# Joining two down projections into one accumulation, and taking two weight scales from column norms

## The chip, the core and the metric

The kernel runs on one core of one Trainium2 chip. The metric is device time in microseconds from one launch to its end, the median of three runs. One further execution was taken with the hardware profiler, and all rows shown below are from it. The engines are named as the profile names them: PE is TensorE (PEld its weight loads), DVE is VectorE, ACT is ScalarE, POOL is GpSimd, and SP is the engine whose queue issues nearly all DMAs here (SPq).

## What is computed

One layer of a pre-normalised residual block over 2048 tokens of width 1024, in float32, with two attention branches (differential attention with 4 heads, stick-breaking attention with 8) and a SwiGLU feed-forward part of 2816 features:

```python
u = rms_norm(h, norm1_w[l])
proj = jnp.einsum('bsd,de->bse', u, w_in[l])
...
h = h + jnp.einsum('bse,ed->bsd', mix, w_out[l])
u2 = rms_norm(h, norm2_w[l])
gate = jnp.einsum('bsd,df->bsf', u2, w_gate[l])
up = jnp.einsum('bsd,df->bsf', u2, w_up[l])
h = h + jnp.einsum('bsf,fd->bsd', jax.nn.silu(gate) * up, w_down[l])
```

The change lies in the last four lines, and in how the operands of `gate` and `up` are prepared.

## The kernel before, in words

Float32 accuracy comes from 16-bit matmuls: each operand is scaled by a power of two and split into a high and a low f16 part, and a product is three matmuls (high·high, high·low, low·high).

The first phase (0 to about 1474 us) does the normalisation, the input projection, both attentions and the output projection. `out_proj` takes the 16 token tiles (128 tokens each) one after the other: 96 matmuls of 128x256 into `po`, the residual is added (`xf`), and the sum goes to the DRAM tensor `hd`. For tiles 0 to 7, `post` also normalises the tile, transposes it on PE, and `x_ops` forms the seven operands X of the next phase, which go to the DRAM tensor `xcd`.

The second phase (1474 to 2866 us) is the feed-forward part: two halves of 1024 tokens, and in each 11 groups of 256 features, so 22 steps. A 2x2 block product is done Strassen-Winograd fashion, with seven block products in place of eight. Step i does on PE

- gate(i): seven products of 12 matmuls of 128x512 (`quad`, `product`), whose results ACT and DVE turn into silu values (tiles `cg`);
- down(i-1): for each of four pairs of token tiles (the loop over `j`), seven products of three matmuls, 84 in all, into PSUM tiles `pd`. DVE adds each one, scaled by `kd`, into `cu` scratch or into the output tiles `hs` (`acc`), and POOL or DVE adds scratch to `hs` (`tt`);
- up(i): as gate, and at its end the seven operands of the next down, `act`, in high and low parts (a copy on ACT, a subtraction on POOL or DVE).

The output tiles `hs`, eight of 128x1024 float32, stay in SBUF through a half: they are loaded from `hd` once, and stored to `out` in its last down.

The weights of a step (`g`, `u`, `d`: 1 MB each) are loaded in float32 into the tag `fst` (two buffers), combined in place on POOL, and split into f16 (`load_ffn`, `split_weight`): high parts on ACT or POOL, low parts on DVE. Gate and up weights share the tag `wgu` (two buffers), `wd` has one. In half 0 each weight first gets its scale from its data. For `g` and `u` that is a maximum of absolute values over 2048 columns on DVE (L190). For `d` it is a sum of squares on ACT (L187), written to the `wd` tile as junk. The 128 partition results are spread by a small float32 matmul into `fsc` (`across`, L179) and reduced once more on DVE. Half 1 uses the scales again. `build_x` makes the X operands of half 1 piece by piece in the downs of half 0 (the `ticks`), in buffers `bx` and `fst`.

The order of the instructions on each engine comes from a scheduler that simulates the program with its buffers, in the order in which the code emits it; `pick` gives a piece of work to the engine that has been given least by `note`. Each engine then runs its own queue in that order, so what waits at a queue's head holds up all behind it.

## Time and profile before

| | |
|---|---|
| median of three runs | 2863.46 us (2859.81 to 2869.82) |
| the profiled execution, its own time | 2867.49 us |
| its span, first to last instruction | 2865.7 us |
| mean granted TensorE clock | 0.957 |
| PE busy | 2510.0 us (88%) |
| DVE busy | 2399.3 us (84%) |
| POOL busy | 1847.9 us (64%) |
| ACT busy | 1469.5 us (51%) |
| gate(0) starts | 1477.07 us |
| first up product of half 0, of half 1 | 1502.22 us, 2174.30 us |
| last down starts | 2838.45 us |

A busy engine in this profile need not be at its peak, and the share of a whole span is an average over stages. The two halves of the feed-forward part show this: the same 252 matmuls per step take 67.2 us in half 0 ((2174.30 − 1502.22) / 10) and 58.05 us in half 1, where no scales are computed and no X operands are built.

### The profile page before, as it was taken

To read this page: it belongs to the slowest core of one execution; us is meant where nothing else is said; L and a number is where in the kernel's file an instruction comes from. 1 tells how busy PE (TensorE), PEld (TensorE's weight loads), DVE (VectorE), ACT (ScalarE), POOL (GpSimd) and SP (SyncE) were. 2 spreads that over 40 slices of the span, in tenths; PEclk is the share of its full clock that TensorE was granted. 3 is DMA by queue.
4 is the path that set the end of the run, shared out by engine and by line. 5 is a ranking of instruction groups with operands and counts; after the bars stand their busy time and mean duration, and the time that the engine had idled before them with its cause. 6 is when DMAs were issued, how large, how long until landed. Compare 5 with 4: busy or idle time off the path is not lost.

```text
span 2865.7 us, 45554 instructions
## 1 busy us (share of the span) xinstructions
PE 2510.0 (88%) x16888; PEld 1396.6 (49%) x16888; DVE 2399.3 (84%) x4152; ACT 1469.5 (51%) x2680; POOL 1847.9 (64%) x1258
## 2 busy tenths in 40 slices
PE   7998898988888777899888989888899999999997
PEld 4565555555555444477653434333344444444443
DVE  6888879787989999787548989889988888898887
ACT  4665656567777888656323433434334333433432
POOL 3567767664545555465427867767777887787775
PEclk9999999999999888999999989999999999999999
DMA  6778877879999898978951222323134511111111
GB/s 229 194 159 176 169 172 161 179 165 220 214 192 192 163 177 167 203 166 225 268 216 44 84 71 76 96 74 94 45 96 162 176 45 59 59 50 54 59 45 59
DMA packets 672224, 390.95 MB, mean 136 GB/s; under 512 B 532784, under 2 KB 622896, under 8 KB 670208
## 3 DMA queue, kind: packets, MB, share of 16 engines
q1 hardware_dynamic: 670176, 385.95, 55.2%
q8 instruction: 132, 2.16, 0.3%
q0 software_dynamic: 512, 1.36, 0.2%
q14 instruction: 92, 0.75, 0.1%
q10 hardware_dynamic: 1312, 0.72, 0.1%
HBM read 199.48 MB, written 49.02 MB: 87 GB/s over the span
## 4 chain that ended last, share of the span: by engine, by line
PE 21%; DVE 18%; POOL 7%; issue 6%; DMA 4%; ACT 2%; SPq 0%; DVEq 0%; POOLq 0%; ACTq 0%
PE pd L975 6%; PE pa L887 4%; PE pm L887 4%; DVE wu L210 4%; PE pd L887 4%; POOL hs L101 2%; POOL fst L101 2%; PE po L752 2%; DVE wg L210 2%; DVE cg L101 2%; DVE hs L984 1%; DVE wd L210 1%; DVE z L553 1%; DVE cu L984 1%; DVE m L190 1%
## 5 line engine op out<-in xcount | busy, mean ns | idle before, releaser
L101 POOL TENSOR_TENSOR s<-z,s 128x1024 f16<-128x1024 f32 (+7 forms) x288 | 472.9, 1650 | 329.8 <-ACT s L92 292.6
L316 PE MATMUL pj<-w,xt 128*128 128x384 f16 x3072 | 577.1, 336 | 24.4 <-DVE st L326 9.1
L975 PE MATMUL pd<-wd,act 128*128 128x512 f16 x1848 | 425.9, 382 | 58.7 <-ACT act L944 17.6
L101 POOL TENSOR_TENSOR fst<-fst 128x512 f32<-128x512 f32 x197 | 341.4, 1734 | 196.2 <-DVE wu L210 69.0
L316 PEld LDWEIGHTS <-xt 128*128 128x128 f16 x3072 | 301.8, 101 | 236.6 <-issue 42.3
L553 DVE TENSOR_TENSOR_SCAN z<-z,sc 128x512 f32<-128x512 f32 (+3 forms) x320 | 355.4, 1113 | 68.5 <-ACT sc L551 64.6
L444 PE MATMUL sc<-kT,qT 128*128 128x512 f16 (+3 forms) x1280 | 349.2, 363 | 72.5 <-DVE z L554 29.1
L101 POOL TENSOR_TENSOR hs<-hs,cu 128x512 f32<-128x512 f32 x258 | 354.8, 1401 | 76.7 <-DVE cu L984 61.1
L454 PE MATMUL yp<-v,aT 128*128 128x64 f16 (+1 forms) x4896 | 284.5, 209 | 76.5 <-DMA aT<-s 76.0
L454 PEld LDWEIGHTS <-aT 128*128 128x128 f16 x4896 | 248.2, 102 | 166.6 <-DMA aT<-s 102.5
L975 PEld LDWEIGHTS <-act 128*128 128x128 f16 x1848 | 180.4, 98 | 291.4 <-issue 59.9
L887 PEld LDWEIGHTS <-wg 128*128 128x128 f16 x1848 | 184.4, 100 | 244.4 <-issue 35.2
L887 PEld LDWEIGHTS <-wu 128*128 128x128 f16 x1848 | 182.9, 99 | 223.1 <-issue 12.1
L984 DVE SCALAR_TENSOR_TENSOR hs<-pd,c,hs 128x512 f32<-128x512 f32 x352 | 247.3, 740 | 24.5 <-PE pd L975 24.5
L92 ACT CAST s<-z 128x384 f16<-128x384 f32 (+7 forms) x216 | 170.2, 789 | 142.7 <-DMA aT<-s 61.3
L550 ACT ACTIVATE z<-sc,c 128x512 f32<-128x512 f32 (+3 forms) x320 | 203.5, 636 | 15.7 <-PE sc L446 10.2
L944 ACT CAST act<-cg 128x512 f16<-128x512 f32 x132 | 81.3, 616 | 240.0 <-DVE cg L101 124.2
L554 DVE TENSOR_TENSOR z<-sc,z 128x512 f32<-128x512 f32 (+3 forms) x320 | 193.1, 606 | 7.7
L101 POOL TENSOR_TENSOR act<-cg,act 128x512 f16<-128x512 f32 x104 | 151.7, 1469 | 69.3 <-ACT act L944 69.3
L551 ACT ACTIVATE sc<-sc,c 128x512 f32<-128x512 f32 (+3 forms) x320 | 195.7, 612 | 0.0
L752 PE MATMUL po<-wo,mt 128*128 128x256 f16 x1536 | 183.4, 277 | 13.2 <-DVE xf L755 12.2
L887 PE MATMUL pm<-X,wg 128*128 128x512 f16 x792 | 179.9, 379 | 0.2 <-ACT wg L205 0.2
(221 smaller groups left out, 4524.7 us busy)
## 6 DMA issues: line engine op xcount, KB each, us to landing
xt<-xs SPq DMA_DIRECT2D x112, 512.0 KB, 4.3
fst<-in_w_gate_dram SPq DMA_DIRECT2D x22, 1024.0 KB, 5.4
fst<-in_w_up_dram SPq DMA_DIRECT2D x22, 1024.0 KB, 5.4
fst<-in_w_down_dram SPq DMA_DIRECT2D x22, 1024.0 KB, 4.9
X<-xcd SPq DMA_DIRECT2D x14, 1024.0 KB, 7.9
wst<-in_w_in_dram SPq DMA_DIRECT2D x24, 512.0 KB, 6.4
z<-in_x_dram SPq DMA_DIRECT2D x16, 512.0 KB, 5.6
xs<-xt SPq DMA_DIRECT2D x16, 512.0 KB, 2.9
```

The costliest lines, as they stand in the source:

```text
L101: (DVE if e == "D" else POOL).tensor_tensor(dst, a_, b_, op)
L210: DVE.scalar_tensor_tensor(lo, st, sW[:], hi, op0=ALU.mult, op1=ALU.subtract)
L316: PE.matmul(pj[:, :384], lhsT=xv[:, xi, kt, :], rhs=G["w"][:, wi, kt, :], start=n == 0, stop=n == 23)
L444: PE.matmul(sc[:, : 128 * w].rearrange("p (t n) -> p t n", n=P), lhsT=G["q"][i // 4][:, 2 - 2 * o + m, i % 4, :], rhs=G["k"][q][:, m, 0:w, ...
L454: PE.matmul(yp[:, y0 : y0 + wd], lhsT=aT[:, a_, :], rhs=v[:, v_ : v_ + wd], start=start and j == 0 and q == 0, stop=stop and j == nb - 1 a ...
L550: ACT.activation(om[:, lo:hi], sc[:, :w], AF.Sigmoid, scale=G["nkz"][:])
L551: ACT.activation(sc[:, :w], sc[:, :w], AF.Sigmoid, scale=G["kz"][:])
L553: DVE.tensor_tensor_scan(ov, ov, sc[:, :w], om[:, hi : hi + 1], op0=ALU.mult, op1=ALU.bypass)
L752: PE.matmul(po[:, sl], lhsT=mt[:, kt, P * xi : P * xi + P], rhs=wos[2 * h + n][wi][:, kt, :], start=q == 0, stop=q == 23)
L887: PE.matmul(ps_[:].rearrange("p (t n) -> p t n", n=P), lhsT=wv[:, wo, wi, 128 * kt : 128 * kt + 128], rhs=X[xo][:, :, xi, kt, :], start=st ...
L975: PE.matmul(po[:], lhsT=act[:, ao, xi, 128 * j : 128 * j + 128], rhs=dv[:, wo, wi, :], start=start and q == 0, stop=q == 2, skip_group_che ...
L984: DVE.scalar_tensor_tensor(dst, po[:], W["kd"][:], src, op0=ALU.mult, op1=ALU.add)
```

## The change

Four things change, all in the second phase but for one line in `out_proj`.

1. **Joined downs.** `act` and `wd` get two buffers each, and `down` takes a list of one or two steps. With two, each PSUM tile accumulates six matmuls in place of three, and is evacuated once, with the `kd` of the later step; the powers of two in `kd` and `F` are set anew. There are 12 downs in place of 22: in steps 2, 4, 6, 8, 10 (two steps each), in step 11 (the one left over of half 0), in steps 13, 15, 17, 19, 21 (two each), and one at the end. The output tiles `hs` have four buffers, two pairs: every down loads them pair by pair from `hd`, and stores them back to `hd`, or to `out` in the half's last down.
2. **Scales from column norms.** For `g` and `u`, ACT squares the 128x2048 weights to bf16 (`sq`, one buffer), PE adds them over partitions with eight accumulating matmuls against a tile of ones, and DVE takes the maximum of 256 columns from PSUM. `d` keeps its path, with `sq` as junk.
3. **Loads in two parts.** `load_ffn` is a generator: its first part issues the DMA and the squares, its second the scale and the split. The parts are emitted inside gate, down and up by hooks.
4. **X operands of half 1.** `post` runs for tiles 0 to 11, so two of the four pairs of half 1 are made in the first phase; `build_x` makes the other two within steps 0 and 1, in the four `hs` buffers and one `act` buffer (`b16`), which step 1's `act` needs next.

```diff
             def load_ffn(half, fg, names, W):
...
                     st = stage(fg, nme, half)
-                    late = nme == "d" and half == 1 and fg == NFG - 1
-                    w16 = fw.tile([P, 7, 2, 512], F16, tag="wd" if nme == "d" and not late else "wgu", bufs=1 if nme == "d" and not late else 2, name=nm("w" + nme))
                     if half == 0:
...
+                        sq = fw.tile([P, 2048], BF16, tag="sq", bufs=1, name=nm("sq"))
+                        if nme == "d":
+                            cols = scale_begin([st[:]], sq[:])
+                        else:
+                            ACT.activation(sq[:], st[:], AF.Square)
+                            note("A", 1900)
+                    yield
+                    late = nme == "d" and half == 1 and fg == NFG - 1
+                    w16 = fw.tile([P, 7, 2, 512], F16, tag="wd" if nme == "d" and not late else "wgu", bufs=2, name=nm("w" + nme))
+                    if half == 0:
                         pt = ps2.tile([P, 512], F32, tag="b", bufs=8, name=nm("fsc"))
-                        weight_scale([st[:]], r[:], p[:], pt, junk, sW)
+
+                        def columns(m):
+                            for k in range(KT):
+                                PE.matmul(pt[:, :256], lhsT=ones[:], rhs=sq[:, 256 * k : 256 * k + 256], start=k == 0, stop=k == KT - 1)
+                            DVE.tensor_reduce(m, pt[:, :256], op=ALU.max, axis=AX.X)
+
+                        scale_end((lambda m: across(m, pt, cols)) if nme == "d" else columns, r[:], p[:], True, sW)
                         sc[nme] = (r, p, sW)
                     sW = sc[nme][2]
```

```diff
                     SP.dma_start(hd[t], xf)
-                    if t >= NT // 2:
+                    if t >= 12:
                         yield
...
-            def quad(wv, X, tag, bufs, c11):
...
+                if hook is not None:
+                    hook()
                 pd = pst("pd")
                 product(pd, wv, 2, X, 2, True, True)
...
-            def up(W, X, sg):
-                act = fp.tile([P, 7, 2, 512], F16, tag="act", bufs=1, name=nm("act"))
+            def up(W, X, sg, hook=None):
+                act = fp.tile([P, 7, 2, 512], F16, tag="act", bufs=2, name=nm("act"))
...
+            def load_hs(half, j):
+                h = [hp.tile([P, D], F32, tag="hs", bufs=4, name=nm("hs")) for _ in range(2)]
+                for q in range(2):
+                    SP.dma_start(h[q][:], hd[8 * half + 2 * j + q])
+                return h
+
+            def down(half, units, hs, last, hook=None):
+                kd = units[-1][0]["kd"]
+                nu = len(units)
 
                 def prod(po, ao, wo, j, start=True):
-                    for q, (xi, wi) in enumerate(((0, 0), (0, 1), (1, 0))):
-                        PE.matmul(po[:], lhsT=act[:, ao, xi, 128 * j : 128 * j + 128], rhs=dv[:, wo, wi, :], start=start and q == 0, stop=q == 2, skip_group_check=not start)
+                    for u, (W, act) in enumerate(units):
+                        for q, (xi, wi) in enumerate(((0, 0), (0, 1), (1, 0))):
+                            PE.matmul(po[:], lhsT=act[:, ao, xi, 128 * j : 128 * j + 128], rhs=W["d"][:, wo, wi, :], start=start and u == 0 and q == 0, stop=u == nu - 1 and q == 2, skip_group_check=not start)
...
                 for j in range(4):
-                    if j in TK:
-                        next(ticks, None)
-                    h0, h1 = hs[j], hs[j + 4]
+                    if j == 2 and hook is not None:
+                        hook()
+                    if j + 1 < 4:
+                        hs.append(load_hs(half, j + 1))
+                    h0, h1 = hs[j]
...
-                    if last:
-                        for k in (j, j + 4):
-                            t = tile_of(k)
-                            SP.dma_start(out[t * P : (t + 1) * P, :], hs[k][:])
+                    for q in range(2):
+                        t = 8 * half + 2 * j + q
+                        SP.dma_start(out[t * P : (t + 1) * P, :] if last else hd[t], hs[j][q][:])
```

```diff
+                w2f, xa, xb, xt = (hp.tile([P, D], F32, tag="hs", bufs=4, name=nm("bx")) for _ in range(4))
+                SP.dma_start(w2f[:], a["norm2_w"].partition_broadcast(P))
+                DVE.tensor_scalar(w2f[:], w2f[:], r_24[:], None, op0=ALU.mult)
+                b16 = fp.tile([P, 7, 2, 512], F16, tag="act", bufs=2, name=nm("b16"))[:].rearrange("p o s n -> p (o s n)")
+                n = [0]
...
+                d2 = lambda z: z[:].rearrange("p (d n) -> p d n", d=2)
+                for j in (2, 3):
+                    for q, z in enumerate((xa, xb)):
+                        SP.dma_start(z[:], hd[8 + 2 * j + q])
                     yield
-
-                def bufs():
-                    b16 = fw.tile([P, 2048], F32, tag="fst", bufs=2, name=nm("xst"))[:].bitcast(F16)
-                    return b16[:, :2048], b16[:, 2048:]
-
-                d2 = lambda z: z[:].rearrange("p (d n) -> p d n", d=2)
-                yield from x_ops([d2(z) for z in xn], d2(xt), 1, j, bufs, "AP", "DP")
+                    for z in (xa, xb):
+                        norm_tile(z[:], z[:], w2f[:], xt[:])
+                        yield
+                    yield from x_ops([d2(z) for z in (xa, xb)], d2(xt), 1, j, bufs, "AP", "DP")
...
+                due = len(units) == 2 or (fg == 0 and units)
+                if due:
+                    dh = steps[i - 1][0]
+                    hs = [load_hs(dh, 0)]
...
+                def in_gate():
+                    begin("g", *steps[i + 1], "g", Wn) if more else None
+                    if i < 2:
+                        tick(2)
+
+                def in_down():
+                    end("g")
+                    begin("d", half, fg, "d", W)
+
+                def in_up():
+                    end("d")
+                    begin("u", *steps[i + 1], "u", Wn) if more else None
+
+                sg = gate(W, X, in_gate)
+                if i < 2:
+                    tick(2 if i == 0 else 16)
...
+                if due:
+                    down(dh, units, hs, dh != half, in_down)
+                    units = []
+                else:
+                    in_down()
+                act = up(W, X, sg, in_up)
+                end("u")
+                if i == 0:
+                    tick(4)
+                units.append((W, act))
+                if not more:
+                    down(half, units, [load_hs(half, 0)], True)
                 W = Wn
```

Two places show how the queues move. The first is SP, at the second half-0 step of before, and at the first joined down of the change. Before, the queue holds little but the weights (`fst`) and the DMAs that build X operands (`xst`, `xcd`):

```order
L816 DMA fst_20355<-in_w_gate_dram 128x8x256
L814 DMA fst_20388<-in_w_down_dram 128x2x1024
L816 DMA fst_20544<-in_w_up_dram 128x8x256
L230 DMA_TRANSPOSE xst_20676<-xst_20676 128x16x128
L231 DMA xcd_82<-xst_20676 128x2x1024
L230 DMA_TRANSPOSE xst_20761<-xst_20761 128x16x128
L1031 DMA bx_21211<-hd 128x1024
```

and now the stores and loads of the output tiles:

```order
L818 DMA fst_20908<-in_w_down_dram 128x2x1024
L1055 DMA hd<-hs_20631 128x1024
L1055 DMA hd<-hs_20630 128x1024
L998 DMA hs_20809<-hd 128x1024
L998 DMA hs_20810<-hd 128x1024
L1055 DMA hd<-hs_20745 128x1024
L1055 DMA hd<-hs_20744 128x1024
L998 DMA hs_20916<-hd 128x1024
L998 DMA hs_20917<-hd 128x1024
L820 DMA fst_21129<-in_w_up_dram 128x8x256
L1055 DMA hd<-hs_20810 128x1024
L1055 DMA hd<-hs_20809 128x1024
```

Each store of a pair (`hd<-hs`) now stands ahead of the load into the same two buffers for a later pair, and the load of the up weights of a later step stands behind two pairs' stores.

The second place is ACT, where the `act` of step 1 is written (the rows with `act_` are its copies, `L90` is the copy into `b16`, `wu`, `wg`, `wd` are weight splits, `cg` are silu values). Before, in step 1:

```order
L944 CAST act_20422<-cg_20139 128x512
L944 CAST act_20422<-cg_20154 128x512
L944 CAST act_20422<-cg_20125 128x512
L900 COPY cg_20586<-pa_20573 128x512
L92 CAST xst_20761<-bx_20188 128x2x512
L205 ACTIVATE wu_20546<-fst_20544,c_20549 128x2x512 x2
L205 ACTIVATE wu_20546<-sx_20560,c_20549 128x512
L944 CAST act_20422<-cu_20531 128x512
L944 CAST act_20422<-cg_20096 128x512
L205 ACTIVATE wu_20546<-fst_20544,c_20549 128x2x512
```

and now, where `act_20444` takes the buffer that `b16_19950` had:

```order
L90 CAST b_19950<-bx_19945 128x512
L959 ACTIVATE cg_20302<-cg_20302,c_20044 128x512
L210 ACTIVATE wu_20212<-fst_20143,c_20147 128x2x512
L210 ACTIVATE wg_20402<-fst_20318,c_20322 128x2x512 x2
L210 ACTIVATE wg_20402<-sx_20419,c_20322 128x512
L959 ACTIVATE cg_20273<-cg_20273,c_20044 128x512
L924 COPY cu_20458<-pa_20445 128x512
L184 ACTIVATE sq_20441,m_20442<-fst_20436 128x2048
L210 ACTIVATE wg_20402<-fst_20318,c_20322 128x2x512
L970 CAST act_20444<-cg_20316 128x512
L210 ACTIVATE wd_20504<-fst_20436,c_20440 128x2x512 x2
```

The square of the down weights (`sq_20441`) now stands ahead of the copies, and their split behind the first of them, which needs the buffer of `b_19950` to be free; the last copy into that buffer is the first row shown.

## The prediction

> **What bounds the kernel now.** I read the stages first (the windows), since the two halves differ, then what PE waits for, then the timeline around the waits.

> Windows of two stretches in half 0 and one in half 1 (busy us of PE, PEld, DVE, ACT, POOL; then clock, DMA share, GB/s):

> ```profile
> core 0: us, PE busy (x) PEld busy (x) DVE busy (x) ACT busy (x) POOL busy (x), PEclk, DMA share, GB/s
> 1600.00:1700.00 100.00, 85.83 (x372) 37.44 (x371) 88.88 (x113) 38.28 (x52) 72.90 (x52) 0.93 0.31 90
> 1700.00:1800.00 100.00, 91.86 (x411) 41.09 (x410) 90.53 (x130) 41.86 (x51) 72.15 (x48) 0.97 0.24 69
> 2300.00:2400.00 100.00, 96.07 (x441) 42.88 (x440) 85.42 (x94) 39.98 (x53) 82.53 (x53) 1.00 0.16 53
> ```

> In half 0 PE and DVE are both near 90%: neither bounds alone, they take turns. In half 1 PE has 96%. The waits of PE over the second phase (total us, times, longest):

> ```profile
> PE fsc L179 <- DVE m L190: 32.8, 11, 7.3
> PE fsc L179 <- ACT wd L187: 22.6, 11, 2.1
> PE pd L975 <- ACT act L944: 17.6, 6, 6.7
> PE pd L975 <- DVE cu L984: 17.3, 14, 2.7
> PE pd L975 <- DVE hs L984: 12.8, 17, 1.5
> PE pd L887 <- DVE cg L915: 11.0, 11, 4.0
> PE pd L975 <- ACT cu L997: 8.9, 12, 0.9
> ```

> 55.4 us go to the scale matmuls (`fsc`), 39.0 to `cu` and `hs` in the downs. PE's timeline around two scale waits and over one down of half 1:

> ```profile
> 1477.07 1.03 PE L887 MATMUL pa<-X,wg 128*128 128x512 f16 x2 [2.19 <-ACT wg L205]
> ...
> 1526.60 0.77 PE L179 MATMUL fsc<-id,m 128*128 128x128 f32 x2 [7.27 <-DVE m L190]
> 1527.16 4.48 PE L887 MATMUL pa<-X,wg 128*128 128x512 f16 x12
> ...
> 1570.41 0.49 PE L179 MATMUL fsc<-id,m 128*128 128x128 f32 x2 [2.09 <-ACT wd L187]
> 1570.73 4.44 PE L887 MATMUL pa<-X,wu 128*128 128x512 f16 x12
> ...
> 1590.29 2.75 PE L887 MATMUL pa<-X,wg 128*128 128x512 f16 x12
> ...
> 2174.30 2.75 PE L887 MATMUL pa<-X,wu 128*128 128x512 f16 x12
> 2176.89 5.34 PE L887 MATMUL pm<-X,wu 128*128 128x512 f16 x24
> ...
> 2189.84 2.54 PE L887 MATMUL pa<-X,wg 128*128 128x512 f16 x11
> ```

> ```profile
> 2512.39 5.35 PE L975 MATMUL pd<-wd,act 128*128 128x512 f16 x24 [1.11 <-DVE cu L984]
> 2518.30 1.47 PE L975 MATMUL pd<-wd,act 128*128 128x512 f16 x6 [0.56 <-DVE hs L984]
> 2520.71 0.81 PE L975 MATMUL pd<-wd,act 128*128 128x512 f16 x3 [0.95 <-ACT cu L997]
> ```

> Twelve matmuls take 2.59 us from start to start (2174.30 to 2176.89), 0.216 each, so a step's 252 are 54.4 us of pure PE. A step lasts 67.2 us in half 0 and 58.05 in half 1 (the table above). The losses are 12.8 and 3.65 us a step: in half 0 scales, the clock after them (12 matmuls in 4.48 where 2.75 is normal) and the downs; in half 1 the downs, where evacuation runs behind PE.

> **The change, part by part.** First whether any engine is fuller than PE afterwards. Groups from 1520 us on (busy us, mean ns):

> ```profile
> L101 POOL TENSOR_TENSOR hs<-hs,cu 128x512 f32<-128x512 f32 x258 | 354.8, 1401 | 76.7 <-DVE cu L984 61.1 <-DVE hs L984 14.9
> L984 DVE SCALAR_TENSOR_TENSOR hs<-pd,c,hs 128x512 f32<-128x512 f32 x352 | 247.3, 740 | 24.5 <-PE pd L975 24.5
> L984 DVE SCALAR_TENSOR_TENSOR cu<-pd,c,cu 128x512 f32<-128x512 f32 x176 | 129.6, 742 | 12.5 <-ACT cu L997 9.1 <-PE pd L975 0.5
> L190 DVE TENSOR_REDUCE m<-fst 128x1 f32<-128x2048 f32 x19 | 43.3, 2278 | 10.6 <-DMA fst<-in_w_gate_dram 9.6 <-DMA fst<-in_w_up_dram 1.0
> L187 ACT ACTIVATE wd<-fst 128x2048 bf16<-128x2048 f32 x10 | 19.1, 1910 | 45.2 <-PE pd L975 45.2
> L179 PE MATMUL fsc<-id,m 128*128 128x128 f32 x58 | 14.4, 334 | 52.8 <-DVE m L190 31.8 <-ACT wd L187 20.9
> ```

> Steps now come in pairs: one without a down, 168 matmuls or 36.3 us, and one with a joined down, 336 matmuls or 72.6 us; 108.9 us of PE together. DVE per pair now: half 0 0.897 x 134.4 = 120.6, half 1 0.854 x 116.1 = 99.1. A removed down takes away 16 accumulations into `hs` and 8 into `cu`, 24 x 0.741 = 17.8; in half 0 the four reductions of a pair go too, 9.1. That leaves DVE about 94 and 81 us, against 108.9 of PE. POOL now has 0.725 x 134.4 = 97.4 and 0.825 x 116.1 = 95.8, and loses some 12 adds of 1.4, 16.8: about 81 and 79. ACT, at 0.40 of 134.4, gains four squares of 1.91: about 61. So PE is alone at the top, and what remains is sequence.

> - **Removed waits in the downs.** A pair j has 42 matmuls, 9.07 us, where it had 4.54, with the same evacuation behind them. The waits of 1.11, 0.56 and 0.95 are lags of about a microsecond of an evacuation that now has twice the time, so I take them as gone in joined downs.
> - **Scales.** PE gets 16 matmuls of 128x256 per step in half 0. The output projection runs such matmuls at 112 ns (5.40 us for 48, below): 1.8 us a step, where four float32 passes of 0.334 go and the two of `d` stay: 2.5 us a step for all scales. The square comes as soon as the DMA lands, and the matmuls that wait for it stand after later PE work. In the step with a down the chain of load and square has 36 us of down matmuls as cover. In the step without one, the `u` load waits until the `g` split has left `fst`; load (5.4 us, in the DMA rows below) and square (1.91) then end about 5 us after PE arrives. Below: 2 (the wait for ACT now). Above: 7.3 (the longest now). I take 5, and 2 more for the clock (4.48 − 2.75).
> **The clock after a wait.** Waits of 7.27 and 2.09 us were each followed by 12 matmuls in over 4.4 us.

> [...]

> - **The output tiles through DRAM.** 80 loads and 80 stores of 512 KB are new. Bounds from the DMA list (KB each, us to landing):

> ```profile
> hd<-xf SPq DMA_DIRECT2D x16, 512.0 KB, 4.9
> hs<-hd SPq DMA_DIRECT2D x16, 512.0 KB, 6.6
> out_dram<-hs SPq DMA_DIRECT2D x16, 512.0 KB, 3.1
> bx<-hd SPq DMA_DIRECT2D x8, 512.0 KB, 4.4
> fst<-in_w_up_dram SPq DMA_DIRECT2D x22, 1024.0 KB, 5.4
> w2f<-in_norm_w_dram SPq DMA_DIRECT2D x1, 512.0 KB, 11.2
> ```

> With two pairs of buffers, a pair must be used, stored and loaded again within the 18.1 us that PE needs for two j. Use is the last five of a pair's seven products, 1.30 us each, and one add of 1.4: 7.9. With a store of 3.1 and a load of 4.4 a turn is 15.4: hidden. With 4.9 and 6.6 it is 19.4: 1.3 late per joined down. I take the first, as nearest to a DMA share of 0.16 to 0.31, and leave up to 1 us in the remaining waits below. A load of 11.2 is the slower rival.
> - **First phase.** `post` for four more tiles adds 32 transposes and their copies on engines that idle there. Rows of the last stretch:

> ```profile
> 1400.00:1475.00 75.00, 63.63 (x593) 54.41 (x591) 16.12 (x29) 1.16 (x3) 3.55 (x3) 0.95 0.66 233
> ...
> 1413.09 5.40 PE L752 MATMUL po<-wo,mt 128*128 128x256 f16 x48
> ...
> L590 PE MATMUL xtr<-id,z 128*128 128x128 f32 x192 | 29.2, 291 | 2.7 <-DVE z L218 1.8 <-DVE xt L609 0.8
> ```

> The transposes take at most 32 x 0.29 = 9.3 us; the X loads also move behind later stores on SP, under a DMA share of 0.66. Below 0, if all of it fills the gaps of the stretch (75 − 63.6 = 11.4 us idle); above 15, the 9.3 and one store of 4.9 that the X loads wait for. I take 6.
> - **Steps 0 and 1**, gate(0) to gate(2), last 113.2 us now (1477.07 to 1590.29). down(0), 84 x 0.216 = 18.1, moves out to a later step; what it leaves is filled in part by the X building, which is packed into these steps: −18 with the X building under cover, 0 where it fills the place. I take −15, since DVE and ACT lose the down's evacuation too.
> - **`act` of step 1** waits for `b16` (the ACT rows above), and the split of the down weights stands behind it. Eight operand builds go through two halves of one buffer, each a transpose through a DMA and a store; at 4.4 and 3.1 us (the nearest rows above) that is a chain of 60 us, about what is left of the two steps: 0 below, 20 above; I take 8.
> - **Steps 2 to 10**, 599.55 us now (1590.29 to 2189.84). Work: nine gate-and-up of 36.3, ten steps' downs of 18.1 and 2.5 a step for the scales: 530. Waits: four steps without a down at 7, and 12 for the rest: 570. So −29.
> - **Half 1**, gate(11) to the last down, 648.6 us now (2189.84 to 2838.45). Work: 11 x 54.4 = 598.4 (one down in, one out). Now 50 us are lost; the down waits shown are 2.62 of 3.65 a step, 29 in 11 steps, so 21 stay, the load of X and the single down of step 11 among them: −29.
> - **The end.** The last down's rows now:

> ```profile
> 2838.45 18.42 PE L975 MATMUL pd<-wd,act 128*128 128x512 f16 x78 [4.73 <-ACT act L944]
> ...
> 2846.76 11.19 POOL L101 TENSOR_TENSOR hs<-hs,cu 128x512 f32<-128x512 f32 x9 [6.43 <-DVE cu L984]
> ```

> It is still single, so PE needs 9.1 us for two j. A turn of 4.7 (use at half the product time) + 3.1 + 4.4 = 12.2 makes it 3 late, one of 19.4 makes it 10 late; I take 7.

> Sum: +6 − 15 + 8 − 29 − 29 + 7 = −52; 2867.5 − 52 = 2815.5 for a profiled execution, and as the median is 4 us below that execution now, **2811 us**. Its own range, from the bounds named, is 2787 to 2834.

> **Rivals.** *The round trip sets the pace* (slower). If loads land in 11.2 us like `w2f`, with stores at 4.9, a turn is 24.0 against 18.1: 5.9 late, once for pairs 2 and 3 together, 59 in ten joined downs; the two single downs, with 9.1 us for a turn, lose 15 each where 7 are counted in one: 23 more. −52 + 59 + 23 = +30: about 2893. It decides from a turn of 21.4 on, where 33 and 19 use up the 52. For it: every store stands ahead of later weight loads on SP, so a late add holds up weights as well. Against it: that row is one transfer, and shares of 0.16 to 0.31 leave the queues mostly empty.

> *Full gain.* No wait is left in steps 2 to 10 (40 better), `b16` and the first phase cost nothing (14), half 1 loses 10 (11): −52 − 65 = −117 at the extreme; halfway, −85, it is 2779. For it: DVE has 15 us to spare per pair. Against: each split's chain is serial on three engines.

> *The scale waits stay.* If `fsc` waits about 12 us in each step without a down and `d`, `g` wait 2 each, steps 2 to 10 lose 28 more: 2839. For it: `fst` still has two buffers. Against: the squares need no DVE.

> *No change:* joined downs come out as a longer wait elsewhere, and DVE's low parts set the pace: it had 89% in half 0. But it loses 27 of 120.6 us a pair, so little is left for this; 2863.

> **How the numbers follow.** Chances: forecast 0.51, full gain 0.15, scale waits 0.17, no change 0.04, round trip 0.13. A measurement of this kernel tells about 0.3% (9 us) from no change. Forecast, full gain and scale waits are all faster: 0.83; the same 0.04; slower 0.13. The range takes in the scale-wait case with its spread and most of the full gain: 2767 to 2860; it leaves out slower, half of no change and a piece of the full gain, about 0.19.

> **What would show it.** Right: pairs of steps of some 120 us in half 0 and 112 in half 1; waits of `pd` for `cu` and `hs` gone; `fsc` waits near 5 us only in steps without a down; `hs` DMA waits on DVE under 1 us; gate(0) near 1483. Wrong: DVE or PE waiting for `hs<-hd` in every joined down; step 1's `act` copy waiting over 20 us for `xcd` stores; `fsc` waits in all steps; or the first phase ending 15 us later.

## The result, and the profile after

The changed kernel takes 2850.27 us (median of seven runs, 2841.08 to 2853.32), beside 2863.46 us for the kernel before: a ratio of 0.9949, 95% interval 0.9933 to 0.9964. It is 0.5% faster, 13 us, where 52 us were forecast. The profiled execution has a span of 2847.8 us beside 2865.7, 17.9 us less.

The first lines of its page (busy time by engine):

```profile
span 2847.8 us, 45790 instructions
PE 2519.3 (88%) x17052; PEld 1409.9 (50%) x17052; DVE 2229.5 (78%) x3922; ACT 1481.5 (52%) x2666; POOL 1703.5 (60%) x1133
```

DVE lost 170 us of busy time and POOL 144: per pair of steps DVE lost about 25 us in half 0 and 13 in half 1, where 27 and 18 had been worked out. That so much engine time was set free, and the kernel's time hardly moved, is the question of this study. What PE waits for in the second phase (columns as in the prediction):

```profile
PE pd L911 <- DVE cg L941: 42.9, 19, 4.9
PE pd L1008 <- DVE hs L1017: 11.2, 5, 4.8
PE pd L1008 <- POOL act L99: 9.3, 4, 3.5
PE fsc L853 <- ACT sq L843: 8.8, 4, 2.9
PE pd L1008 <- ACT act L970: 6.2, 3, 4.7
...
PE fsc L177 <- ACT sq L184: 5.6, 3, 2.2
...
PE pd L1008 <- DVE cu L1017: 2.6, 1, 2.6
```

The waits for scales went from 55.4 us to 14.4 (and one of 3.9 for the tile of ones, ahead of gate(0)), those of the downs for `cu` and `hs` from 39.0 to 13.8 (and 0.4 for ACT's `cu`). In their place stands a line that was 11.0 us: a product of the gate (`pd L911`) waits 42.9 us for DVE to read its first half out of PSUM, the memory that PE writes its products to (`cg L941`). Such a read is called an evacuation here. The stage borders, from PE's timeline:

```profile
1482.83 4.84 PE L911 MATMUL pa<-X,wg 128*128 128x512 f16 x12
...
1585.10 2.75 PE L911 MATMUL pa<-X,wg 128*128 128x512 f16 x12
...
2151.26 2.54 PE L911 MATMUL pa<-X,wg 128*128 128x512 f16 x11
...
2812.20 18.93 PE L1008 MATMUL pd<-wd,act 128*128 128x512 f16 x72 [4.73 <-ACT act L970]
```

These are gate(0), gate(2), gate(11) and the last down. Set against the terms of the prediction:

| stage | before, us | after, us | measured | predicted |
|---|---|---|---|---|
| up to gate(0) | 1477.1 | 1482.8 | +5.8 | +6 |
| gate(0) to gate(2) | 113.2 | 102.3 | −10.9 | −15 + 8 = −7 |
| gate(2) to gate(11) | 599.6 | 566.2 | −33.4 | −29 |
| gate(11) to the last down | 648.6 | 660.9 | **+12.3** | **−29** |
| the last down to the end | 27.3 | 35.6 | +8.3 | +7 |

Four of five terms hold within 5 us. The whole miss is half 1, which got slower although it computes no scales and builds nothing. There a pair of steps is now, for instance, 36.8 and 78.7 us long, where 36.3 and 72.6 are pure PE: the step without a down is nearly perfect (36.3 to 37.5), the step with one loses 6 to 8 us (steps 13 to 19: 28.8 in all). Step 11, with the single down of half 0, takes 68.4 us where 54.4 are pure PE and it took 58.2 before. PE's timeline over step 15, with a down:

```profile
2371.43 2.75 PE L911 MATMUL pa<-X,wg 128*128 128x512 f16 x12
...
2385.43 2.75 PE L911 MATMUL pd<-X,wg 128*128 128x512 f16 x12
...
2393.05 0.60 PE L1008 MATMUL pd<-wd,act 128*128 128x512 f16 x2 [0.34 <-ACT act L970]
2398.52 4.36 PE L911 MATMUL pd<-X,wg 128*128 128x512 f16 x12 [4.87 <-DVE cg L941]
2402.72 26.06 PE L1008 MATMUL pd<-wd,act 128*128 128x512 f16 x120
2428.95 6.85 PE L1008 MATMUL pd<-wd,act 128*128 128x512 f16 x31 [0.16 <-DVE hs L1017]
```

The gate's product of 2385.43 is ready at about 2388. It has to be read before PE adds the next product to the same PSUM tile, and PE gets that at 2398.5. DVE's queue in between:

```profile
2388.92 3.43 DVE L99 TENSOR_TENSOR cg<-cg,cg 128x512 f32<-128x512 f32 x2
2392.27 0.68 DVE L931 TENSOR_TENSOR cg<-pm,cg 128x512 f32<-128x512 f32 x1
2392.87 1.04 DVE L99 TENSOR_TENSOR cg<-cg,cg 128x512 f32<-128x512 f32 x1
2393.83 2.28 DVE L215 SCALAR_TENSOR_TENSOR wu<-fst,c,wu 128x1024 f16<-128x1024 f32 x1
2396.04 1.64 DVE L99 TENSOR_TENSOR act<-cg,act 128x512 f16<-128x512 f32 x1
2397.78 0.69 DVE L941 TENSOR_TENSOR cg<-pd,cg 128x512 f32<-128x512 f32 x1
```

`L941` waits for nothing in its own right; it stands in the queue behind the last split of this step's up weights (`wu L215`), which nobody needs for another 40 us, and behind operands of this step's down. After the wait 12 matmuls take 4.36 us in place of 2.75, so the price is some 6.5 us at this place alone.

Steps 19 and 21 wait the same 4.87 us for the same evacuation. In steps 13 and 17 PE stops a few matmuls earlier, 3.5 us each, for the low part of `act`, which POOL makes out of sums that DVE computes in the same queue:

```profile
2281.45 1.04 PE L1008 MATMUL pd<-wd,act 128*128 128x512 f16 x4 [3.52 <-POOL act L99]
```

Engine time is not short on average. Two windows, the step without a down with the turn into the next, and the down:

```profile
2337.54:2400.00 62.46, 56.36 (x257) 25.11 (x256) 52.19 (x45) 28.83 (x39) 46.77 (x27) 0.99 0.20 66
2400.00:2455.00 55.00, 54.84 (x250) 24.58 (x249) 34.70 (x40) 13.11 (x18) 32.91 (x22) 0.98 0.57 194
```

DVE (the third pair) is 84% busy in the first and 63% in the second. Three weights are now split in the 36 us of PE work of a step without a down, where before the same three had the 54 us of every step. The DMA share of the second, 0.57, is mostly the round trip of the output tiles (8 stores and 8 loads of 512 KB, beside two weights of 1 MB).

### The profile page after: what moved, and what is told of

Its sections match the earlier page's. It is cut to its first block, busy times and chain, and to the rows that moved or that the text cites. A ratio compares the mean times of both kernels' runs of the same rounds, so it can differ in the third digit from the quotient of the medians.

```text
span 2847.8 us, 45790 instructions
## 1 busy us (share of the span) xinstructions
PE 2519.3 (88%) x17052; PEld 1409.9 (50%) x17052; DVE 2229.5 (78%) x3922; ACT 1481.5 (52%) x2666; POOL 1703.5 (60%) x1133
## 4 chain that ended last, share of the span: by engine, by line
PE 21%; DVE 16%; DMA 7%; POOL 6%; issue 5%; ACT 3%; SPq 1%; DVEq 0%; POOLq 0%; ACTq 0%
PE pd L1008 11%; DVE wu L215 3%; PE pd L911 3%; POOL fst L99 3%; PE pm L911 3%; PE pa L911 3%; DVE wd L215 2%; DVE cg L99 2%; DMA fst<-in_w_down_dram 2%; DVE cg L976 1%; PE po L757 1%; DVE z L558 1%; DMA aT<-s 1%; DMA xcd<-b 1%; DMA b<-b 1%
## 5 line engine op out<-in xcount | busy, mean ns | idle before, releaser
L99 POOL TENSOR_TENSOR fst<-fst 128x512 f32<-128x512 f32 x193 | 348.3, 1805 | 225.2 <-DVE wg L215 98.0
L1008 PE MATMUL pd<-wd,act 128*128 128x512 f16 x1848 | 416.2, 384 | 30.0 <-DVE hs L1017 11.2
L449 PE MATMUL sc<-kT,qT 128*128 128x512 f16 (+3 forms) x1280 | 347.2, 362 | 72.7 <-DVE z L559 26.3
L911 PEld LDWEIGHTS <-wg 128*128 128x128 f16 x1848 | 185.8, 101 | 279.3 <-issue 76.2
L911 PEld LDWEIGHTS <-wu 128*128 128x128 f16 x1848 | 182.1, 99 | 231.7 <-issue 19.2
L99 POOL TENSOR_TENSOR hs<-hs,cu 128x512 f32<-128x512 f32 x138 | 190.6, 1391 | 165.4 <-DVE cu L1017 66.4
L90 ACT CAST s<-z 128x384 f16<-128x384 f32 (+7 forms) x216 | 170.4, 790 | 139.2 <-DMA aT<-s 59.0
L1017 DVE SCALAR_TENSOR_TENSOR hs<-pd,c,hs 128x512 f32<-128x512 f32 x192 | 139.0, 745 | 131.0 <-PE pd L1008 98.6
L99 POOL TENSOR_TENSOR act<-cg,act 128x512 f16<-128x512 f32 x108 | 173.2, 1609 | 103.1 <-ACT act L970 103.1
L757 PE MATMUL po<-wo,mt 128*128 128x256 f16 x1536 | 184.2, 279 | 13.0 <-DVE xf L760 12.5
L970 ACT CAST act<-cg 128x512 f16<-128x512 f32 x132 | 80.5, 615 | 212.1 <-DVE cg L976 124.8
L911 PE MATMUL pm<-X,wg 128*128 128x512 f16 x792 | 178.6, 379 | 1.0 <-POOL wg L214 1.0
## 6 DMA issues: line engine op xcount, KB each, us to landing
xt<-xs SPq DMA_DIRECT2D x112, 512.0 KB, 4.2
hs<-hd SPq DMA_DIRECT2D x96, 512.0 KB, 4.3
hd<-hs SPq DMA_DIRECT2D x80, 512.0 KB, 5.1
fst<-in_w_gate_dram SPq DMA_DIRECT2D x22, 1024.0 KB, 5.1
fst<-in_w_up_dram SPq DMA_DIRECT2D x22, 1024.0 KB, 5.3
fst<-in_w_down_dram SPq DMA_DIRECT2D x22, 1024.0 KB, 4.8
X<-xcd SPq DMA_DIRECT2D x14, 1024.0 KB, 9.6
wst<-in_w_in_dram SPq DMA_DIRECT2D x24, 512.0 KB, 6.5
```

The lines of the kernel that those rows point to most:

```text
L90: ACT.copy(dst, src)
L99: (DVE if e == "D" else POOL).tensor_tensor(dst, a_, b_, op)
L449: PE.matmul(sc[:, : 128 * w].rearrange("p (t n) -> p t n", n=P), lhsT=G["q"][i // 4][:, 2 - 2 * o + m, i % 4, :], rhs=G["k"][q][:, m, 0:w, ...
L757: PE.matmul(po[:, sl], lhsT=mt[:, kt, P * xi : P * xi + P], rhs=wos[2 * h + n][wi][:, kt, :], start=q == 0, stop=q == 23)
L911: PE.matmul(ps_[:].rearrange("p (t n) -> p t n", n=P), lhsT=wv[:, wo, wi, 128 * kt : 128 * kt + 128], rhs=X[xo][:, :, xi, kt, :], start=st ...
L1008: PE.matmul(po[:], lhsT=act[:, ao, xi, 128 * j : 128 * j + 128], rhs=W["d"][:, wo, wi, :], start=start and u == 0 and q == 0, stop=u == nu ...
```

## The experiments

An experiment's code is cut to its main lines, with `...` for what is left out; where a text says "gate(i)" or "step i", i counts from 0 to 21, and half 1 begins with step 11. Theory A: the steps without a down have too much on DVE's queue, in the wrong order; the split of the up weights in front of the gate's evacuation is what PE waits for. Theory B, the slower rival of the prediction: the round trip of the output tiles sets the pace. A further question is what each half of the change is worth alone. Ratios are to the kernel before on the same chip; the changed kernel has 0.9949.

**1. No round trip.** Two pairs of output buffers stay through a half, and the pairs 2 and 3 are added into those of 0 and 1: the kernel leaves out the loads and stores between, and its sums are mixed.

```diff
+                if (half, j % 2) in kept:
+                    return kept[half, j % 2]
...
-                    for q in range(2):
+                    for q in range(2) if last else ():
```

> The changed kernel, but the output tiles make no round trip: two pairs of buffers are loaded once per half, stay, and are stored only in the half's last down (pairs 2 and 3 are added into the buffers of pairs 0 and 1, so the sums over tiles are mixed; all other work is the same). Theory A (the steps without a down are overfull: three weights are split in 36 us of PE time, and the split of the up weights stands in DVE's queue ahead of the gate's evacuation): pairs of steps in half 1 stay at 116 to 118 us, and only the lateness at the two single downs goes, some 5 to 12 us in all: 2838 to 2846. Theory B (the round trip of the output tiles through DRAM is what DVE, POOL and then PE wait for): pairs in half 1 fall to about 111, half 0 gains too: 2810 to 2825.

Measured: 2847.92 us, 0.993 (0.9909 to 0.9951), the intervals overlap with the changed kernel's. The eight steps from gate(13) to gate(21) take 468.3 us beside 467.6. From gate(11) to the last down it takes 661.0 us beside 660.9. So theory B, alone, does not explain the miss; only the last step and the end became 5.7 us shorter. The round trip is not without waits in the changed kernel, though. DVE, over the second phase:

```profile
DVE hs L1017 <- DMA hs<-hd: 32.3, 11, 5.3
```

They lie in the downs of steps 10, 11, 13, 15, 17 and 21, and run 1, which has none of them, is no faster in half 1 (run 9 comes back to this).

**2. Late up weights.** In a step with a down, the up weights are loaded in the gate and their split is emitted in the down's first pair.

```diff
                 def in_gate():
-                    begin("g", *steps[i + 1], "g", Wn) if more else None
+                    if due:
+                        begin("u", half, fg, "u", W)
+                    else:
+                        begin("g", *steps[i + 1], "g", Wn) if more else None
...
+                def at_start():
+                    end("u")
+                    begin("g", *steps[i + 1], "g", Wn) if more else None
```

> The changed kernel, but the up weights of a step that has a down are loaded during that step's gate and split in its down's first pair, in place of the step before; the load of the next gate weights follows them. Theory A (overfull steps without a down): the wait of the gate's pd product for DVE's evacuation (42.9 us over 19 times) and most of the cold clock after it go; pairs in half 1 fall from 117 to about 111 or 112, in half 0 from 122 to about 118: 2795 to 2820. Theory B (round trip): no change, 2843 to 2855, or slower by the DVE work added beside the late loads.

Measured: 2837.17 us, 0.9887 (0.9866 to 0.9908): faster than the changed kernel, but not by what theory A gave. All of the gain is in half 0 (gate(2) to gate(11) 547.4 us beside 566.2), where the split needs a scale, and that comes from matmuls in PE's own order. In half 1, where it needs nothing but the DMA, the scheduler put it where it had been, ahead of the evacuation, and PE waits the same 4.87 us in step 15: 473.9 us for the eight steps. The edit did not do there what it was for.

**3. Joined downs alone**, with the scales of before.

```diff
-                        else:
-                            ACT.activation(sq[:], st[:], AF.Square)
...
+                        cols = scale_begin([st[:]], sq[:] if nme == "d" else None)
...
-                        scale_end((lambda m: across(m, pt, cols)) if nme == "d" else columns, r[:], p[:], True, sW)
+                        scale_end(lambda m: across(m, pt, cols), r[:], p[:], nme == "d", sW)
```

> The changed kernel with the scales of gate and up weights as before: DVE takes the maximum of absolute values (2.28 us each), a small float32 matmul spreads it; no squares, no column sums. If the prediction's term for half 0 is made by the column norms: DVE gets 9.1 us per pair more where it is 77% busy, and the scale matmuls wait again for DVE: half 0 10 to 25 us slower, 2860 to 2875. If joining alone made it: 2846 to 2855. Half 1 must be the same as in the changed kernel (pairs 115 to 118 us), since no scales are made there.

Measured: 2837.61 us, 0.9891 (0.9870 to 0.9913). This is neither of the expectations: without the column norms the kernel is 0.6% *faster* than with them, 16 us in the profiles' steps 2 to 10 (550.3 beside 566.2), and half 1 is unchanged (466.2 beside 467.6). From step 4 on, the steps of half 0 with a down take 72.3 us here and 76 to 77 in the changed kernel; the others 47 in both, on average.

**4. The new scales alone**, on the kernel before, with the squares as junk in the weight's own buffer.

```diff
-                        weight_scale([st[:]], r[:], p[:], pt, junk, sW)
...
+                            ACT.activation(sq, st[:], AF.Square)
+                            for k in range(KT):
+                                PE.matmul(pt[:, :256], lhsT=ones[:], rhs=sq[:, 256 * k : 256 * k + 256], start=k == 0, stop=k == KT - 1)
...
```

> The kernel before, with only the scales changed: squares on ACT written as junk into the weight's own f16 buffer (there is no room for another), eight matmuls with ones, maximum over 256 columns. 22 reductions of 2.28 us leave DVE, in half 0 only. If DVE's reductions are what half 0 waits for: steps there fall from 67.2 to about 64 us, 2825 to 2845. If the square's wait for the weight buffer takes its place, as the down weights' square shows with 2.1 us a time: 2855 to 2870. Half 1 unchanged at 58 us a step.

Measured: 2881.82 us, 1.0047 (1.0030 to 1.0063), slower, and above the upper expectation. The longest new waits of PE in its half 0 were 21.4 us for the square of the up weights (ten times) and 34.9 us for DVE's evacuation in up (tile `cu`):

```profile
PE pd L901 <- DVE cu L929: 34.9, 10, 6.1
PE fsc L841 <- ACT wu L838: 21.4, 10, 3.0
```

22 reductions of 2.28 us left DVE and bought nothing: the scale was late by another engine, and an evacuation came late. What the square's wait for its buffer has in this can't be told apart from the rest here.

**5. Ordered up splits.** As run 2, and the low-part splits of those up weights are ordered behind the gate's last evacuation on DVE's own queue.

```diff
+            if behind[0] is not None:
+                tc.add_manual_dep(lo_op.ins, behind[0].ins.name, ..., reason="issue order")
...
+                    behind[0] = evac[0]
                     end("u")
+                    behind[0] = None
```

> The run with late up weights showed 1.1% less time than before, all of it in half 0: in half 1 the scheduler still put the up split of a step with a down ahead of that step's gate evacuations on DVE (steps with a down 81 to 83 us there). Here these low-part splits are ordered behind the gate's last evacuation on DVE's queue; nothing else is different. Theory A (the split that stands in front is what makes PE wait for the gate's evacuation and for the low parts of act): steps with a down in half 1 fall from 80.5 to about 73 us, 35 us over five of them, and the waits of pd for cg and act in half 1 (about 33 us) nearly vanish: ratio to before about 0.975 to 0.982. Rival (the operands act are late by their own chain over ACT, DVE and POOL, or the up split then comes too late for the up products): half 1 stays above 79 us per such step, or up waits for wu, ratio 0.986 to 0.995.

Measured: 2812.73 us, 0.9801 (0.9783 to 0.9819). PE and DVE at the same turn of half 1, gate start 2348.22:

```profile
2362.37 2.75 PE L915 MATMUL pd<-X,wg 128*128 128x512 f16 x12
...
2369.92 2.75 PE L915 MATMUL pd<-X,wg 128*128 128x512 f16 x12
2372.51 28.01 PE L1012 MATMUL pd<-wd,act 128*128 128x512 f16 x129
2403.60 4.91 PE L1012 MATMUL pd<-wd,act 128*128 128x512 f16 x22 [3.08 <-DVE hs L1021]
```

```profile
2365.84 0.88 DVE L99 TENSOR_TENSOR act<-cg,act 128x512 f16<-128x512 f32 x1
2366.83 0.69 DVE L945 TENSOR_TENSOR cg<-pd,cg 128x512 f32<-128x512 f32 x1
...
2373.31 2.48 DVE L217 SCALAR_TENSOR_TENSOR wu<-fst,c,wu 128x1024 f16<-128x1024 f32 x2
```

The evacuation (`L945` here) comes 18.6 us after the gate's start in place of 26.3, and PE passes without a wait. In half 1 the wait for `cg` falls from 19.1 to 2.9 us and that for `act` (POOL and ACT) from 14.2 to 4.7, the one ahead of the last down. Against run 2, which has the same loads and the same work, nothing but the order differs: the ratio goes from 0.9887 to 0.9801. This shows theory A's order. But the steps with a down fall to 78 us and not to 73: a wait of 3.08 us stands late in the down, for `hs` (0.16 in the changed kernel), and behind it DVE, over half 1:

```profile
DVE hs L1021 <- DMA hs<-hd: 40.7, 11, 5.7
```

**6. The same order without column norms** (the edits of runs 3 and 5 together), **7. that kernel with another order of pairs** (the single down of half 1 in step 12, so that the last one is joined), and **8. one matmul per column norm** in place of eight in the changed kernel.

```diff
-                due = len(units) == 2 or (fg == 0 and units)
+                due = len(units) == 2 or (fg == 0 and units) or (half == 1 and fg == 1)
```

```diff
-                            for k in range(KT):
+                            for k in range(1):
```

> The same ordering of the up splits, with the scales as before the change (DVE's reductions, no column sums). If the column norms cost what the run without them showed (0.9949 against 0.9891) and this adds to the ordering: about 0.005 below the ordering with column norms, 0.970 to 0.977. If the column norms cost only through the queue order that is now mended, the two are equal within 0.002.

> The run before this one, with the single down of half 1 in step 12 and pairs after it, so that the last down is a joined one of 36 us and not a single one whose third pair waits for a reload. If the reload is what the single down at the end loses (waits of 4.8 and 3.4 us for hs): 5 to 8 us less than the run before this one. If the end only grows with the longer last down: equal, or up to 5 us more.

> The changed kernel with one matmul per column norm in place of eight (the norm is over the first 128 rows of the weight alone, so the scale differs). The column norms cost 16 us as a whole. If that is their time on PE (7 x 14 x 0.112 us per weight, two weights in 11 steps): 12 to 17 us less than the changed kernel, ratio about 0.989 to 0.990. If it is the queue order and the latency of square, sum and maximum: within 5 us of the changed kernel, 0.993 to 0.996.

Measured: without column norms 0.9838 (0.9822 to 0.9855), 2823.32 us; with the other order of pairs 0.9812 (0.9795 to 0.9828), 2815.08 us, the intervals of the two overlap; one matmul 0.9951 (0.9935 to 0.9967), 2855.82 us. So in the ordered kernel the column norms *gain* 0.4%, where in the changed kernel they cost 0.6%. Their sign hangs on the queue order, and less on their own work: leaving out seven of eight matmuls changes the total by nothing that can be measured. (Its steps 2 to 10 are 8 us shorter, 557.8, and the rest 14 us longer with the same code, so up to half of the cost could still be PE's time.) The rows show the order. The changed kernel, DVE at a gate of half 0 that starts at 2074.12:

```profile
2094.98 1.28 DVE L215 SCALAR_TENSOR_TENSOR wu<-fst,c,wu 128x1024 f16<-128x1024 f32 x1 [2.33 <-ACT wu L210]
2096.18 0.68 DVE L941 TENSOR_TENSOR cg<-pd,cg 128x512 f32<-128x512 f32 x1
```

and joined downs alone, gate start 2068.64:

```profile
2086.58 0.69 DVE L929 TENSOR_TENSOR cg<-pd,cg 128x512 f32<-128x512 f32 x1 [1.05 <-POOL act L99]
2087.38 0.69 DVE L933 TENSOR_TENSOR cg<-cg,pm 128x512 f32<-128x512 f32 x1
2090.11 1.28 DVE L215 SCALAR_TENSOR_TENSOR wu<-fst,c,wu 128x1024 f16<-128x1024 f32 x1 [2.04 <-ACT wu L210]
```

The last up split stands ahead of the gate's evacuation in the one, and waits there 2.33 us for ACT while DVE is free; in the other it stands behind. PE waits 4.3 us in the first and not at all in the second.

**9. Ordered, without round trip.**

> The run with the ordered up splits, and the output tiles without round trip (two pairs of buffers stay for a half, pairs 2 and 3 are added into those of pairs 0 and 1, so the sums over tiles are mixed). In that run DVE waits 40.7 us in half 1 for loads of hs, PE 22.4 behind it, and steps with a down take 78 us where 72.6 are pure PE. If the round trip is now the bound that the queue order hid before: steps with a down at 73 to 74 us, 4 to 5 us less in each of ten, ratio 0.965 to 0.972 against 0.980. If the waits only move again: 0.977 to 0.981, as little as the 0.2% that the same edit brought to the changed kernel itself.

The edit is that of run 1 on the kernel of run 5, with its mixed sums. Measured: 2784.31 us, 0.9701 (0.9678 to 0.9724). The steps with a down in half 1 take 73.7 us, 73.6, 73.8, 72.7. The first stretch of them, PE first:

```profile
2186.20:2300.00 113.80, 112.79 (x524) 50.93 (x523) 93.55 (x94) 43.03 (x56) 84.69 (x54) 1.00 0.29 93
```

PE is busy 99% there. The round trip costs 28 us in the ordered kernel, all in half 1 (gate(2) to gate(11) is 548.4 beside 548.9), and some 5 us in the changed one (run 1). That the loads there have time to land because PE stops for the evacuation anyway is our reading of the two pairs of runs.

One turn of the tiles in the ordered kernel, in step 15 of run 5:

```profile
2379.60 1.40 DVE L1021 SCALAR_TENSOR_TENSOR hs<-pd,c,hs 128x512 f32<-128x512 f32 x2
2389.39 1.19 SPq L1061 DMA_DIRECT2D hd<-hs  x2
2394.59 0.57 SPq L1002 DMA_DIRECT2D hs<-hd  x1
2402.79 1.41 DVE L1021 SCALAR_TENSOR_TENSOR hs<-pd,c,hs 128x512 f32<-128x512 f32 x2 [5.17 <-DMA hs<-hd]
```

From the first use of the first pair to the landing of the pair that takes its buffers it is 23.1 us: 10.6 until the second store is issued, 3.7 for that store, 0.7 until the load is issued, and 8.1 until it has landed.

**10. Ordered, with the other order of pairs** (edit of run 7), and **11, 12. all adds into the output tiles on DVE**, on the kernels of runs 5 and 10.

```diff
-LE, SE, AE = "DP", "D", "P"
+LE, SE, AE = "DP", "D", "D"
```

> The ordered up splits, and the single down of half 1 in step 12 with pairs after it. On the kernel without column norms this order of pairs brought 0.26%. If it adds: ratio 0.9765 to 0.9785 against 0.9801, about 2806 us and the fastest so far. If the two interfere in steps 11 to 13, where two single downs now follow each other: 0.979 to 0.982.

> The ordered up splits, and all adds of scratch into the output tiles on DVE in place of POOL (12 a down, 0.7 to 1.0 us each there, 1.27 to 2.26 on POOL). The round trip costs the ordered kernel about 28 us; a pair of tiles can be stored only after its last add. If a shorter turn of the tiles is worth something: PE's waits for hs in half 1 fall from 22 us to under 12, ratio 0.975 to 0.978. If DVE's extra 10 us per down delay its accumulations instead: 0.980 to 0.986.

> The same adds on DVE, with the single down of half 1 in step 12. If both small gains add: 0.974 to 0.977, about 2800 us; if the adds on DVE cost more than the turn gains: 0.979 to 0.984.

Measured: 2807.51 us, 0.9786 (0.9762 to 0.9809), for the other order of pairs; with the adds on DVE 0.9822 (0.9803 to 0.9842) and 0.9813 (0.9798 to 0.9828). The order of pairs may bring 0.15%, inside the intervals. The adds on DVE bring nothing: in run 11 DVE's waits for loads of `hs` in half 1 fell from 40.7 to 32.1 us, but PE's waits for `hs` rose from 22.4 to 28.5. That the accumulations come later behind the added work on DVE would explain both; it was not tested.

Of the runs that compute the layer in full, 5 and 10 are the fastest. Stage by stage, from the timelines of the profiled executions (us):

| kernel | gate(0) at | gate(0)–(2) | (2)–(11) | (11)–(13) | (13)–(21) | (21)–end |
|---|---|---|---|---|---|---|
| before | 1477.1 | 113.2 | 599.6 | 116.2 | 465.5 | 94.1 |
| changed | 1482.8 | 102.3 | 566.2 | 105.2 | 467.6 | 123.8 |
| 1 no round trip | 1485.7 | 105.1 | 565.9 | 103.3 | 468.3 | 118.1 |
| 2 late up weights | 1487.6 | 99.6 | 547.4 | 105.6 | 473.9 | 123.1 |
| 3 joined downs alone | 1481.1 | 109.7 | 550.3 | 104.6 | 466.2 | 124.0 |
| 4 new scales alone | 1480.4 | 121.0 | 607.0 | 116.3 | 464.8 | 94.9 |
| 5 ordered | 1487.3 | 96.4 | 548.9 | 101.8 | 460.1 | 117.1 |
| 6 ordered, old scales | 1481.6 | 97.8 | 562.7 | 102.3 | 452.5 | 119.3 |
| 9 ordered, no round trip | 1488.7 | 97.6 | 548.4 | 97.9 | 442.2 | 110.4 |

Rows 5 and 6 differ by 7.6 us from gate(13) to gate(21), where their code is the same: an edit in half 0 also shifts what the scheduler does later, and differences of that size in half 1 are not read as effects.

## Why the prediction was wrong, point by point

**The failing step** is the term for half 1, "so 21 stay, ...: −29", which came out at +12.3, 41 us off; the sum missed by 34 in the spans. Its reasoning had two parts. The first was right for the joined downs: their waits, 2.62 us a step, did go. In the pair that starts at 2371.43 one of 0.16 is left. (The single down of step 11 has 5.2 us of them.) The second was the sentence "So PE is alone at the top, and what remains is sequence", worked from engine time *per pair of steps*: DVE 81 against PE 108.9. DVE measured 87.3 of 118 in the pair that starts at 2371.43, so that was near. But a pair average hides that the weights of a step without a down are split in 36 us and that the DVE time set free lies in the next 36, in the down, where DVE then idles (98.6 us over the second phase, waiting for PE's `pd`). DVE kept to the order of its queue even where it stood idle (at 2094.98 it had waited 2.33 us for ACT, while the operands of `L941` behind it were there from 2091.58 on), and so this became a late evacuation, or a late operand of the down, at the turn between the two: 6 to 8 us per pair with the slow clock behind the wait (a granted clock of 0.50 from 2398.41 to 2401.83). The prediction then costed "sequence" as a remainder, 21 us, taken from the losses before, while the change had moved every split to another place.

The runs divide the 41 us. The stretch of this term, gate(11) to the last down:

| kernel | us | beside 648.6 before |
|---|---|---|
| forecast | 619.6 | −29 |
| changed | 660.9 | +12.3 |
| 1 no round trip | 661.0 | +12.4 |
| 5 ordered | 643.3 | −5.3 |
| 9 ordered, no round trip | 621.4 | −27.2 |

The queue order is 17.6 us of the miss, with the later loads of run 2, which alone gain nothing in half 1. The round trip is another 21.9, and shows only once the order is mended. Both are well above the 7.6 us that are not read as effects. So a second step failed with it, the one that took the round trip as hidden: a turn of 15.4, where run 5 has 23.1. The use was 10.6 and not 7.9 (between the pair's accumulations DVE runs three weight splits, 5.5 us), and one load took 8.1 and not 4.4.

Run 5 as a whole has a ratio of 0.9801, where the forecast of 2811 was 0.982. That this agrees is luck: half 1 is still 24 us short of its term there, and half 0 is 22 us ahead of its own (548.9 us from gate(2) to gate(11), where 570 were forecast).

**Half 0** came out right, 33 us for 29, by other waits than foreseen. The `fsc` waits "near 5 us only in steps without a down" were 2.9 at most, 14.4 in all with those of `d`; the wait for the gate's evacuation, not foreseen, made 23.8 us from gate(0) to gate(11). Two errors offset each other, which is luck, and run 3 shows that a third stood behind: the column norms cost 16 us where the sum had them as a gain. Run 6 against run 5 shows that they gain 14 us in steps 2 to 10 once the order is mended. (The table ahead of the prediction calls 2174.30 us the first up product of half 1; it is that of step 10, the last of half 0. The 67.2 us a step that are drawn from it hold.)

**The round trip** in the changed kernel: loads land in 4.3 us (median), near the 4.4 taken, and stores in 5.1, above the upper bound of 4.9. With use of 7.9 a turn is 17.3 against 18.1, hidden on paper; for PE it was nearly hidden there (run 1). But the sign that was named, "`hs` DMA waits on DVE under 1 us", failed: they are 32.3 us in 11 waits, up to 5.3. That the round trip costs 28 us once PE runs on time (run 9) was in the rivals only as a slower result, not as what limits the gain.

**First phase, steps 0 and 1, the end**: +5.8, −10.9 and +8.3 for +6, −7 and +7. At the end PE waits 4.8 and 3.4 us for `hs`, and DVE, before it, 2.7 and 1.4 for reloads, as foreseen; run 1, which reloads nothing, still has one wait of 3.6 there, so the reload is not all of it.

**The rivals.** Round trip as the pace: not in the changed kernel; in half 1 of run 5 it limits. (By its own terms that rival begins at a turn of 21.5, not 21.4.) Full gain: no. Scale waits that stay: no, though its 2839 is nearest to the time. No change: its words "a longer wait elsewhere" are what half 1 shows, but it laid this to DVE's load, and was given 0.04 because that load falls. None named a queue order that moves with the change. That was the rival to have: in the rows of before, the same `wu` split stands ahead of the same evacuation in half 1, with about no room to spare:

```profile
2499.26 1.27 DVE L210 SCALAR_TENSOR_TENSOR wu<-fst,c,wu 128x1024 f16<-128x1024 f32 x1
2500.46 0.68 DVE L915 TENSOR_TENSOR cg<-pd,cg 128x512 f32<-128x512 f32 x1
```

It is 19.9 us after that gate's start (2480.53), and PE's next product on that tile begins at 2501.19. In step 15 of the changed kernel the same evacuation comes 26.3 us after the gate's start: six microseconds more work ahead of it became some five of wait.

**Chances.** The sign was right; 0.5% is more than the 0.3% that the measurement can't tell from no change. The time lies inside the range, but at its far side, and outside the forecast's own range of 2787 to 2834. Of the signs, gate(0) at 1482.8 and pairs of 120 to 125 us in half 0 came as named; pairs in half 1 are 115 to 118 where 112 were named.

## What to carry to other kernels

When a change moves work between steps, add up each engine for the stretch in which the work must now be done, not for the period; then take the first instruction that PE waits for at the border of the stretches, and list what stands ahead of it in its queue. A greedy scheduler places work as soon as its inputs are there, so emitting it later need not move it (run 2, half 1: the same wait of 4.87 us); an order on the engine's queue does (run 5: PE's waits for `cg` in half 1 from 19.1 to 2.9 us). And a part of a change can have either sign, depending on an order that another part sets: test the parts again once the order is mended (0.6% cost, then 0.4% gain; no cost of the round trip in half 1, then 21.9 us).

## What the runs showed of the hardware

```profile
2171.36 0.60 PE L1008 MATMUL pd<-wd,act 128*128 128x512 f16 x2 [1.17 <-ACT act L970]
2172.92 2.57 PE L1008 MATMUL pd<-wd,act 128*128 128x512 f16 x6 [0.95 <-POOL act L99]
2176.88 4.26 PE L911 MATMUL pd<-X,wg 128*128 128x512 f16 x12 [1.38 <-DVE cg L941]
```

The same stretch by windows (us, PE busy, granted clock, then DMA):

```profile
2169.72:2173.13 3.41, 1.29 (x6) 1.00 0.00 0
2173.13:2176.55 3.42, 2.37 (x6) 0.50 0.00 0
2176.55:2179.96 3.41, 3.08 (x8) 0.50 0.91 308
2179.96:2183.37 3.41, 3.41 (x18) 1.00 0.00 0
```

PE is idle for 2.12 us of the first window, the two waits together, and the next runs at half the clock (0.50). Going through all such windows of this run from 1490 us on: the 18 at full clock in which PE is idle for 2.02 us or more are each followed by one at 0.50, and none of those with 2.00 or less is. In the kernel before, the border lies between 1.93 and 2.09. The wait of 2.09 us in the prediction fits this: it lies whole within the window from 1568.18 to 1571.59, and the next has 0.50.
